# A hybrid decoder layer on one core: transfers ordered with few outstanding, squares on another engine, statistics by block, and one turn of the probabilities moved

## The chip, the cores and the metric

The kernel runs on one core of a Trainium2 chip. The core has TensorE (PE, the matrix multiplications), VectorE (DVE), ScalarE (ACT) and GpSimd (POOL), and SyncE (SP), which issues the transfers; 16 DMA engines carry them out. The metric is the device time of one launch in microseconds.

## The reference

Input x has 2048 rows of 1024 numbers in fp32, mem has 256 rows. The layer computes:

```
h = rms_norm(x, mix_norm_g); z = h @ w_in
lru_x, lru_gate, conf_a, conf_b = split(z)              # 512 columns each
y_lru = rg_lru(causal_dwconv(lru_x, 4 taps)) * gelu(lru_gate)
c = conf_a * sigmoid(conf_b)
c = silu(layer_norm(causal_dwconv(c, 31 taps)))
x = x + concat([y_lru, c]) @ w_out
q = rms_norm(x, xa_norm_g) @ w_q ; k, v = split(rms_norm(mem, mem_norm_g) @ w_kv)
x = x + softmax(q k^T / 16) v @ w_o                     # 4 heads of 256
g, u = split(rms_norm(x, ffn_norm_g) @ w_up)            # 3072 columns each
x = x + (gelu(causal_dwconv(g, 3 taps)) * u) @ w_down
return rms_norm(x, final_norm_g)
```

`rms_norm` divides a row by the root of the mean of its squares and multiplies by a gain; `rg_lru` is a gated linear recurrence along the rows, with two small matrix products for its gates.

## The kernel before, in words

**Numbers and products.** Every fp32 operand of a product is held as two rounded parts, `xh` and `xl` for activations, `wh` and `wl` for weights; ACT rounds (`yh<-s`), and DVE forms the rest (`yl<-s,yh`). `mm3` (line 636) turns one product into three matmuls. Large products are done as seven products of quarter blocks instead of eight (`seven`, line 1178, with the orders FIRST, SECOND and THIRD at 1153 to 1157), and the sums and differences of blocks that this needs (`t`, `s`, `raw`) are DVE's work; the weights' ones are stored in DRAM and read again.

**Stages.** The rows are done in four quarters `q` of 512 and two halves `h` of 1024. `mix_x` (771) loads a quarter of x, takes the sum of squares of its eight 128x512 blocks through `Stats.add` (on ACT, output `junk`), gets 1/rms from ACT's square root and DVE's reciprocal, scales the blocks on ACT (`x<-x,small`) and has PE turn them (`ps<-ident,x`). `memory_a` (1024) does the same for mem, and folds the key weights into w_q and the value weights into w_o. PE then makes z; the values `conf_a * sigmoid(conf_b)` are the tile `sg`, which goes to the DRAM tensor `zc` and comes back with its 30 earlier columns as `z<-zc` for the 31-tap convolution (`conv`, 893). There ACT writes the first tap of three sums (`e<-z`, `so<-z`, `f<-so`), and DVE adds the other taps, `e<-z,v,e` and its kin: this convolution is DVE's largest work in the first third. The recurrence (`lru`) has the tiles `xc`, `gate`, `m`. `attend(h)` (1323) makes three products with `seven`: FIRST (the output projection, into x), SECOND (the scores), and THIRD (probabilities by folded values). Row `score` (around 1388) of SECOND writes or adds to `prob`, and `softmax` exponentiates it on ACT (`prob,small<-prob,...`, with a row sum), takes a reciprocal on DVE and scales on ACT (`prob<-prob,small`). `turn` has PE transpose a block (`ps<-ident,prob`), and ACT copies it out (`pt<-ps`); from `pt` ACT and DVE make the parts `yh` and `yl` of the third product. The dictionary given to `seven` tells after which step (product n, block i) such a side task goes: before, the quarter `(0,0)` of the probabilities is turned after (3, 3), the end of the fourth of the seven score products. The feed-forward part (`feed_forward`, 1790) is a long even run of products with transfers beside them; `finish` (1742) squares the result, takes the statistics of the four blocks `tb` of 512 rows together, and scales and stores them.

**The order.** No engine's order is written by hand. The functions only record operations with what they read and write (`Program`, line 162); tasks are generators that `drive` (537) steps. `deadlines` (277) gives each operation a due time, worked back from PE's order; `schedule` (308) is a list scheduler which, whenever an engine is free in its model, starts the ready operation that is due first, with 85 tile slots S, 4 W, 3 D and 8 PSUM banks. This is repeated PASSES times, and the best of the orders by its own model is emitted. All transfers are issued by SP in one order; an SP entry that waits for its data holds up those behind it, as an ACT or DVE entry does on its engine.

Of the kernel before, what the change touches and what calls it, by code (L numbers as in the profile page):

```python
# [11 lines left out]
F32 = mybir.dt.float32  # L12
F32R = mybir.dt.float32r
AF = mybir.ActivationFunctionType
ALU = mybir.AluOpType
AX = mybir.AxisListType

P = 128
S = 2048
D = 1024  # L20
# [5 lines left out]
NTB = TT // P  # L26
# [12 lines left out]

SLOTS = dict(S=85, W=4, D=3, ps=8)
WIDTH = dict(S=TT, W=1024, D=1152, ps=TT)


# [8 lines left out]
ACT_SWITCH = 1.3  # L54
ACT_PATIENCE = 8.0
POOL_LAST = 6.0
PASSES = 3
STACKS = 2


# [88 lines left out]

class Op:  # L150
    __slots__ = ("eng", "idx", "calls", "cost", "delay", "sets", "preds", "succs", "bufs", "due",
                 "wait", "at", "start", "either", "on", "turn", "store", "first")

    def __init__(self, eng, idx):
        self.eng, self.idx = eng, idx
        self.calls, self.cost, self.delay, self.sets = [], 0.0, 0.0, None
        self.preds, self.succs, self.bufs = set(), [], []
        self.due, self.wait, self.at, self.start, self.either, self.on = 1e9, 0, 0.0, None, False, eng
        self.turn, self.store, self.first = 0.0, False, False


class Program:
# [114 lines left out]
    def deadlines(self, order):  # L277

        t = 0.0
        for o in self.ops:  # L280
            o.due, o.start, o.at = 1e9, None, 0.0
        for o in order:
            if o.eng == "PE":
                o.due = o.turn = t
                t += o.cost
            elif o.store:
                o.due = t + 30
        for o in reversed(self.ops):
            lat = o.cost + o.delay + HOP
            for s in o.succs:  # L290
                o.due = min(o.due, s.due - lat)
            for s in self.extra.get(o.idx, ()):
                if s.idx > o.idx:
                    o.due = min(o.due, s.due - lat)
            if o.first:
                o.due = o.idx - 1e6
        for _ in range(STACKS):
            for e in ("DVE", "ACT", "SP"):
                t = 1e9
                for o in sorted((o for o in self.ops if o.eng == e and not o.first), key=lambda o: -o.due):  # L300
                    t = o.due = min(o.due, t - o.cost)
            for o in reversed(self.ops):
                lat = o.cost + o.delay + HOP
                if o.eng != "PE" and not o.first:
                    for s in o.succs:
                        o.due = min(o.due, s.due - lat)

    def schedule(self):
# [6 lines left out]
        table, dma_free, lag = [None], [0.0], [0.0]  # L315
        order = []

        def push(t, kind, x):
            seq[0] += 1
            heapq.heappush(events, (t, seq[0], kind, x))  # L320
# [49 lines left out]
        def dispatch(e, t):  # L370
            if not idle[e]:
                return
            o = pick(e, t)
            if o is None:
                return
            idle[e] = False
            o.start, o.on = t, e
            order.append(o)
            if e == "PE":
                lag[0] += 0.2 * (t - o.turn - lag[0])  # L380
            cost = o.cost
            if e == "ACT" and o.sets is not None and table[0] not in o.sets:
                cost += ACT_SWITCH
                table[0] = o.sets[0]
            if o.either and e == "DVE":
                cost = estimate("DVE", "tensor_tensor", 1024, False)
            if e == "SP":
                dma_free[0] = max(dma_free[0], t) + cost
                push(t + 0.1, 2, e)
                push(dma_free[0] + o.delay, 0, o)  # L390
            else:
                push(t + cost, 2, e)
                push(t + cost, 0, o)
# [12 lines left out]
        while events:  # L406
            t, _, kind, o = heapq.heappop(events)
# [67 lines left out]
def hybrid_layer(  # L475
# [8 lines left out]
    cpool = ctx.enter_context(tc.tile_pool(name="cpool", bufs=1))  # L484
# [8 lines left out]
    pr = Program(nc, place)  # L493

    def const(shape, name, dtype=F32):
        return Buf(None, shape, cpool.tile(list(shape), dtype, name=name), dtype, name)

    def V(name, *a, **k):
        pr.do("DVE", name, *a, **k)

    def ACT(out, in_, func, **k):
        pr.do("ACT", "activation", out, in_, func, **k)
# [17 lines left out]
    def tmp(name="tmp"):  # L520
        return pr.new("S", name=name)
# [41 lines left out]
    eps = Buf(None, (P, 1), eps_t)  # L563
# [6 lines left out]
    gtail = zeros(NF, FK - 1, "gtail")  # L570
    hlast = zeros(NC4, 1, "hlast")

    n_small = [0]

    def small(w):
        n_small[0] += 1
        return const((P, w), f"small{n_small[0]}")


    def columns(rows, width, name):  # L580
# [119 lines left out]
    class Columns:  # L700
# [6 lines left out]
        def get(self, c0, kq):  # L707
# [10 lines left out]
                        self.kept.put(base + 2 * f + i, flat(got[f][i]))  # L718
            return got

    class Stats:
        def __init__(self):
            self.ss = small(2 * NTB)

        def add(self, tb, half, src):
            i = half * NTB + tb
            ACT(tmp("junk")[:], src, AF.Square, accum_out=self.ss[:, i : i + 1])

        def rstd(self):
            r = small(NTB)  # L730
# [6 lines left out]
    def turn(p, xs, k):  # L737
        with together():
            for tb in range(NTB):
                transpose(p[:, tb * P : (tb + 1) * P], xs[tb][k // 4][:, (k % 4) * P : (k % 4 + 1) * P], ident[:])  # L740
# [30 lines left out]
    def mix_x(h):  # L771
        if h:
            yield mixed_in[0]
        for q in range(2 * h, 2 * h + 2):
            xs = load_x(q, "x")
            st = Stats()
            for tb in range(NTB):
                for half in range(2):
                    st.add(tb, half, xs[tb][half][:])
            r = st.rstd()  # L780
            for half in range(2):
                for tb in range(NTB):
                    t = xs[tb][half]
                    ACT(t[:], t[:], AF.Copy, scale=r[:, tb : tb + 1])
            yield 0
            X = []
            MX[h].append(X)

            def take(k, p):
                hi, lo = pair("x")  # L790
                split_scaled(p[:], vec["v1024"][:, k, G_MIX : G_MIX + 1], hi[:], lo[:])
                X.append((hi, lo))

            yield from turned(xs, take, 1)
            del xs, X

    class Rowed:
# [6 lines left out]
        def put(self, c, q, src):  # L804
            self.tok[c, q] = Buf(None, (1,))
            pr.dma(self.t[c * P : (c + 1) * P, q * TT : (q + 1) * TT], src, writes=[self.tok[c, q]])

        def get(self, out, c, t0, n):
            toks = [self.tok[c, q] for q in range(t0 // TT, (t0 + n - 1) // TT + 1)]
# [214 lines left out]
    def memory_a():  # L1024
        pr.first = True
        xs = []
        for mb in range(2):
            parts = []
            ssp = small(2)
            for half in range(2):  # L1030
                t = tmp("mem")
                pr.dma(t[:], mem[0, mb * P : (mb + 1) * P, half * TT : (half + 1) * TT])
                ACT(tmp("junk")[:], t[:], AF.Square, accum_out=ssp[:, half : half + 1])
                parts.append(t)
            r = small(1)
            V("tensor_tensor", r[:], ssp[:, 0:1], ssp[:, 1:2], op=ALU.add)
            ACT(r[:], r[:], AF.Sqrt, bias=eps[:], scale=1.0 / D)
            V("reciprocal", r[:], r[:])
            for t in parts:
                ACT(t[:], t[:], AF.Copy, scale=r[:, 0:1])  # L1040
            xs.append(parts)
# [281 lines left out]
    def attend(h, ready):  # L1323
# [25 lines left out]
        def turn(src, th, half, take):  # L1349
            for k in range(KH):  # L1350
                p = ps()
                with together():
                    for tb in range(NTB):
                        transpose(p[:, tb * P : (tb + 1) * P], src[th, tb, half][:, k * P : (k + 1) * P], ident[:])
                take(th, half, k, p)
# [37 lines left out]
        def take_p(th, half, k, p):  # L1393
# [5 lines left out]
            (0, 1): [lambda: turn(xs, 1, 0, take), rates],  # L1399
            (1, 3): pass_on(1).get(0, ()),  # L1400
            (3, 0): pass_on(1).get(1, ()),
            (3, 3): [lambda: turn(prob, 0, 0, take_p)],
        })
        del X
        st2 = [Stats(), Stats()]
# [336 lines left out]
    def finish(h, acc):  # L1742
        g = []
        for half in range(2):
            t = tmp("gfin")
            pr.dma(t[:], final_norm_g[half * TT : (half + 1) * TT].partition_broadcast(P))
            g.append(t)
        for th in range(2):
            st = Stats()
            for tb in range(NTB):  # L1750
                for half in range(2):
                    st.add(tb, half, acc[th, tb, half][:])
            r = st.rstd()
            for tb in range(NTB):
                r0 = (2 * h + th) * TT + tb * P
                for half in range(2):
                    t = acc[th, tb, half]
                    V("scalar_tensor_tensor", t[:], t[:], r[:, tb : tb + 1], g[half][:], op0=ALU.mult, op1=ALU.mult)
                    pr.dma(out[0, r0 : r0 + P, half * TT : (half + 1) * TT], t[:])
            yield 1  # L1760

# [107 lines left out]
```

## Time and profile before

| | |
|---|---|
| median of three runs | 2477.26 us (2477.25 to 2478.92) |
| profiled execution | 2480.82 us, of which its span is 2479.0 us |
| PE busy | 2411.2 us (97%), 10788 matmuls |
| DVE busy | 1915.0 us (77%), 3187 instructions |
| ACT busy | 1290.1 us (52%), 2259 instructions |
| DMA moved | 572.06 MB, mean 231 GB/s |

The span is the time from the first to the last instruction of the profiled execution; 1.8 us of its time lie outside of it, and this execution took 3.6 us more than the median. PE is busy for 97% of the span, so the 67.8 us in which it is idle, and the stretches in which its clock is below full, are all that a change of order can win, as long as the matmuls stay the same. Almost all instructions are recorded by one helper, so all carry line 447; they are told apart by their tiles (`ps<-ident,prob` is the turn of the probabilities). In a row of the trace, a bracket at the end is the idle time of that engine before the instruction, and what ended it.

### The profile page before, as it was taken

How to read it: one execution, taken by the hardware profiler on the slowest of the kernel's cores; microseconds unless marked ns; L12 is line 12 of the kernel's file. 1: busy time of each engine (PE TensorE's matmuls, PEld its weight loads, DVE VectorE, ACT ScalarE, POOL GpSimd, SP SyncE). 2: the span in 40 equal slices, each digit the busy share in tenths (PEclk: the TensorE clock that was granted, in tenths of full speed). 3: DMA queues.
4: the chain of work that ended last, by engine and by line, in shares of the span. 5: the costliest groups of instructions: out<-in, count | busy, mean ns of one | idle time of the engine just before them, and what ended most of it. 6: DMA issues, size and time to landing. Idle time of an engine off the chain costs nothing.

```text
span 2479.0 us, 32376 instructions
## 1 busy us (share of the span) xinstructions
PE 2411.2 (97%) x10788; PEld 1986.0 (80%) x10788; DVE 1915.0 (77%) x3187; ACT 1290.1 (52%) x2259; POOL 0.7 (0%) x6
## 2 busy tenths in 40 slices
PE   6999999999989999999999999999999999999998
PEld 5888868877767888778888888888888888888886
DVE  4559979999989635696889888988786685667665
ACT  8427669266977655666545445554454441233222
POOL 0000000000000000000000000000000000000000
PEclk8999999999999999999999999999999999999999
DMA  7977678897796966565665446654542387769774
GB/s 252 378 274 239 217 234 301 267 336 244 234 313 219 374 228 229 157 218 187 235 228 188 171 173 206 223 181 160 173 143 77 102 303 257 257 223 374 255 244 156
DMA packets 339837, 572.06 MB, mean 231 GB/s; under 512 B 32924, under 2 KB 106652, under 8 KB 339670
## 3 DMA queue, kind: packets, MB, share of 16 engines
q1 hardware_dynamic: 339670, 570.00, 67.8%
q8 instruction: 85, 1.39, 0.2%
q14 instruction: 82, 0.67, 0.1%
HBM read 385.32 MB, written 184.55 MB: 230 GB/s over the span
## 4 chain that ended last, share of the span: by engine, by line
PE 68%; DVE 6%; ACT 3%; DMA 1%; issue 1%; SPq 0%; DVEq 0%; ACTq 0%
PE ps L447 68%; ACT prob L447 2%; DVE yl L447 1%; DVE s L447 1%; DVE t L447 1%; DVE gate L447 0%; DVE x L447 0%; DMA wh<-w_out 0%; DMA VO<-yh 0%; DVE Xl L447 0%; ACT yh L447 0%; DVE small L447 0%; DVE prob L447 0%; DVE xc L447 0%; DVE wl L447 0%
## 5 line engine op out<-in xcount | busy, mean ns | idle before, releaser
L447 PE MATMUL ps<-Xh,wh 128*128 128x512 f32 x1344 | 523.9, 390 | 1.1 <-DVE gb L447 0.9
L447 PE MATMUL ps<-Xh,wl 128*128 128x512 f32 x1344 | 523.2, 389 | 0.5 <-DVE wl L447 0.5
L447 PEld LDWEIGHTS ps<-Xh,wh 128*128 128x128 f32 x1344 | 252.3, 188 | 53.9 <-issue 1.3
L447 PEld LDWEIGHTS ps<-Xh,wl 128*128 128x128 f32 x1344 | 252.3, 188 | 53.3 <-DVE wl L447 1.1
L447 PE MATMUL ps<-wh,yh 128*128 128x512 f32 x672 | 268.7, 400 | 11.1 <-ACT yh L447 5.0
L447 PE MATMUL ps<-wh,yl 128*128 128x512 f32 x672 | 265.3, 395 | 2.0 <-DVE yl L447 2.0
L447 PE MATMUL ps<-wl,yh 128*128 128x512 f32 x672 | 264.9, 394 | 0.0
L447 PE MATMUL ps<-wh,hidh 128*128 128x512 f32 x672 | 261.4, 389 | 0.0
L447 PE MATMUL ps<-wl,hidh 128*128 128x512 f32 x672 | 261.4, 389 | 0.0
L447 DVE TENSOR_TENSOR acc<-acc,ps 128x512 f32<-128x512 f32 x192 | 129.2, 684 | 151.4 <-PE ps L447 150.6
L447 PE MATMUL ps<-wh,hidl 128*128 128x512 f32 x624 | 242.7, 389 | 0.0
L447 PE MATMUL ps<-Xl,wh 128*128 128x512 f32 x576 | 224.3, 389 | 1.3 <-DVE Xl L447 1.2
L447 PE MATMUL ps<-xh,wh 128*128 128x512 f32 x512 | 201.7, 394 | 0.0
L447 PE MATMUL ps<-xh,wl 128*128 128x512 f32 x512 | 199.3, 389 | 0.0
L447 PE MATMUL ps<-xl,wh 128*128 128x512 f32 x512 | 199.3, 389 | 0.0
L447 ACT ACTIVATE wh<-s 128x512 fp32r<-128x512 f32 x192 | 120.3, 629 | 133.0 <-DVE s L447 94.4
L447 PEld LDWEIGHTS ps<-wh,yh 128*128 128x128 f32 x672 | 128.5, 191 | 39.9 <-ACT yh L447 5.9
L447 ACT ACTIVATE u<-ps 128x512 f32<-128x512 f32 x144 | 85.6, 595 | 128.4 <-PE ps L447 127.7
L447 PEld LDWEIGHTS ps<-wh,yl 128*128 128x128 f32 x672 | 128.2, 191 | 30.3 <-DVE yl L447 3.0
L447 ACT ACTIVATE wh<-raw 128x512 fp32r<-128x512 f32 x176 | 108.3, 626 | 81.9 <-PE ps L447 43.0
L447 PEld LDWEIGHTS ps<-wl,yh 128*128 128x128 f32 x672 | 128.5, 191 | 27.0 <-issue 0.8
L447 PE MATMUL ps<-xn,wh 128*128 128x512 f32 x384 | 149.4, 389 | 0.0
(208 smaller groups left out, 4546.6 us busy)
## 6 DMA issues: line engine op xcount, KB each, us to landing
raw<-in_w_up_dram SPq DMA_DIRECT2D x96, 512.0 KB
wh<-w_down SPq DMA_DIRECT2D x164, 256.0 KB
wl<-w_down SPq DMA_DIRECT2D x164, 256.0 KB
hid<-cv SPq DMA_DIRECT2D x48, 512.0 KB
h<-hid SPq DMA_DIRECT2D x96, 256.0 KB
w_down<-wh SPq DMA_DIRECT2D x84, 256.0 KB
x<-in_x_dram SPq DMA_DIRECT2D x64, 256.0 KB
wh<-w_out SPq DMA_DIRECT2D x56, 256.0 KB
```

Source lines behind the costliest of these rows:

```text
L447: getattr(e, name)(*[resolve(a) for a in args], **{k: resolve(a) for k, a in kw.items()})
```

## The change

The diff has six parts.

- **Planner.** PASSES goes from 3 to 12. In `deadlines` the due times of PE's operations come from their starts in the schedule before instead of the sum of PE's costs. In `schedule`, SP takes up its next transfer only when the model's backlog of transfers is at most BACKLOG = 4 us. This rule stands in the planner's model only; the emitted kernel has no wait for it.
- **Early stores.** The stores of `sg` to `zc` get a due time that is 40 us earlier.
- **Small tiles.** About a hundred small constants become columns of one tile `smalls`, and the room gives one more slot (S 86).
- **Squares.** The sums of squares of the first quarter of x (8) and of half of each block of mem (2) go to DVE, as `scalar_tensor_tensor` with an accumulated sum, instead of ACT's `Square`.
- **Last norm.** `finish` takes its statistics for each block of 128 rows, not for four together.
- **Turn.** The first quarter of the probabilities is turned after (6, 0), the first block of the seventh score product, instead of after (3, 3).

```diff
-SLOTS = dict(S=85, W=4, D=3, ps=8)
+SLOTS = dict(S=86, W=4, D=3, ps=8)
...
-PASSES = 3
+PASSES = 12
+BACKLOG = 4.0
+EARLY_STORE = 40.0
+SMALLS = 720
...
-        for o in self.ops:
-            o.due, o.start, o.at = 1e9, None, 0.0
         for o in order:
             if o.eng == "PE":
-                o.due = o.turn = t
+                t = o.due = o.turn = t if o.start is None else o.start
                 t += o.cost
-            elif o.store:
-                o.due = t + 30
+            else:
+                o.due = t + 30 if o.store else 1e9
+        for o in self.ops:
+            o.start, o.at = None, 0.0
         for o in reversed(self.ops):
             lat = o.cost + o.delay + HOP
+            if o.early:
+                o.due -= EARLY_STORE
...
             if e == "SP":
                 dma_free[0] = max(dma_free[0], t) + cost
-                push(t + 0.1, 2, e)
+                push(max(t + 0.1, dma_free[0] - BACKLOG), 2, e)
...
     def small(w):
-        n_small[0] += 1
-        return const((P, w), f"small{n_small[0]}")
+        at, n_small[0] = n_small[0], n_small[0] + w
+        assert n_small[0] <= SMALLS, n_small
+        return Buf(None, (P, w), smalls[:, at : at + w], F32, f"small{at}")
...
+    def square(src, total, vector):
+        if vector:
+            V("scalar_tensor_tensor", tmp("junk")[:], src, 1.0, src, op0=ALU.mult, op1=ALU.mult, accum_out=total)
+        else:
+            ACT(tmp("junk")[:], src, AF.Square, accum_out=total)
...
-                    st.add(tb, half, xs[tb][half][:])
+                    st.add(tb, half, xs[tb][half][:], q == 0)
...
+            pr.ops[-1].early = self is zc
...
-                ACT(tmp("junk")[:], t[:], AF.Square, accum_out=ssp[:, half : half + 1])
+                square(t[:], ssp[:, half : half + 1], half == 1)
...
-            (3, 3): [lambda: turn(prob, 0, 0, take_p)],
+            (6, 0): [lambda: turn(prob, 0, 0, take_p)],
...
         for th in range(2):
-            st = Stats()
             for tb in range(NTB):
+                ss, r = small(2), small(1)
                 for half in range(2):
-                    st.add(tb, half, acc[th, tb, half][:])
-            r = st.rstd()
-            for tb in range(NTB):
+                    square(acc[th, tb, half][:], ss[:, half : half + 1], False)
+                V("tensor_tensor", r[:], ss[:, :1], ss[:, 1:], op=ALU.add)
+                ACT(r[:], r[:], AF.Sqrt, bias=eps[:], scale=1.0 / D)
+                V("reciprocal", r[:], r[:])
...
-                    V("scalar_tensor_tensor", t[:], t[:], r[:, tb : tb + 1], g[half][:], op0=ALU.mult, op1=ALU.mult)
+                    V("scalar_tensor_tensor", t[:], t[:], r[:], g[half][:], op0=ALU.mult, op1=ALU.mult)
```

The emitted orders show it at three places. The first is ACT at the start of the program, before: `junk<-x` are the squares of x, `small_97` and `small_109` the square roots for the first and the second quarter, `x<-x,small` the scaling, `xh<-ps` the rounding of the turned x.

```order
20 L447 ACTIVATE kv<-ps 128x256
21 L447 ACTIVATE small_97<-small_97,eps 128x4
22 L447 ACTIVATE junk,small_108<-x 128x512
23 L447 ACTIVATE kv<-ps 128x256
24 L447 ACTIVATE x<-x,small_97 128x512 x4
25 L447 ACTIVATE junk,small_108<-x 128x512
26 L447 ACTIVATE x<-x,small_97 128x512
27 L447 ACTIVATE xh<-ps,v_95 128x512 x2
28 L447 ACTIVATE junk,small_108<-x 128x512
29 L447 ACTIVATE x<-x,small_97 128x512 x3
30 L447 ACTIVATE xh<-ps,v_95 128x512
31 L447 ACTIVATE junk,small_108<-x 128x512
```

The same place on ACT in the changed kernel:

```order
5 L452 ACTIVATE mem<-mem,smalls 128x512 x4
6 L452 ACTIVATE mt<-ps,v_96 128x256 x8
7 L452 ACTIVATE smalls<-smalls,eps 128x4
8 L452 ACTIVATE x<-x,smalls 128x512 x7
9 L452 ACTIVATE xh<-ps,v_96 128x512 x2
10 L452 ACTIVATE x<-x,smalls 128x512
11 L452 ACTIVATE xh<-ps,v_96 128x512
12 L452 ACTIVATE junk,smalls<-x 128x512
13 L452 ACTIVATE xh<-ps,v_96 128x512
14 L452 ACTIVATE junk,smalls<-x 128x512
```

The squares of the first quarter are gone from ACT, all eight scalings of it stand right behind the square root, and the squares of the second quarter come behind them.

The second place is ACT where the first product of the recurrence's input ends (`z<-ps`) and the 31-tap convolution begins (`e<-z`, `so<-z`, `f<-so`), before:

```order
89 L447 ACTIVATE yh<-raw 128x512
90 L447 ACTIVATE sg<-ps 128x512 x4
91 L447 ACTIVATE wh<-raw 128x512 x8
92 L447 ACTIVATE z<-ps 128x512
93 L447 ACTIVATE e<-z,v_102 128x512
94 L447 ACTIVATE so<-z,v_102 128x513
95 L447 ACTIVATE f<-so,fast 128x512
96 L447 ACTIVATE e<-z,v_102 128x512
97 L447 ACTIVATE z<-ps 128x512 x2
```

And in the changed kernel:

```order
84 L452 ACTIVATE yh<-t 128x512
85 L452 ACTIVATE wh<-raw 128x512
86 L452 ACTIVATE e<-z,v_97 128x512
87 L452 ACTIVATE wh<-raw 128x512
88 L452 ACTIVATE so<-z,v_97 128x513
89 L452 ACTIVATE f<-so,fast 128x512
90 L452 ACTIVATE wh<-raw 128x512
91 L452 ACTIVATE z<-ps 128x512
92 L452 ACTIVATE wh<-raw 128x512
93 L452 ACTIVATE z<-ps 128x512
```

Before, the convolution's first taps stand behind `z<-ps`; now they stand ahead of it.

The third place is ACT in the third product of the second half (`attend(1)`), where four blocks of turned probabilities are copied out (`pt<-ps` x4) of which the next parts `yh<-s` are made, before; `prob,small_230<-prob` and its like are the last eight exponentials.

```order
783 L447 ACTIVATE prob,small_230<-prob,small_229,small_177 128x256
784 L447 ACTIVATE prob,small_227<-prob,small_226,small_177 128x256
785 L447 ACTIVATE prob,small_224<-prob,small_223,small_177 128x256
786 L447 ACTIVATE prob,small_221<-prob,small_220,small_177 128x256
787 L447 ACTIVATE prob,small_230<-prob,small_229,small_177 128x256
788 L447 ACTIVATE prob,small_227<-prob,small_226,small_177 128x256
789 L447 ACTIVATE prob,small_224<-prob,small_223,small_177 128x256
790 L447 ACTIVATE prob,small_221<-prob,small_220,small_177 128x256
791 L447 ACTIVATE pt<-ps 128x512 x4
792 L447 ACTIVATE prob<-prob,small_230 128x256
793 L447 ACTIVATE prob<-prob,small_227 128x256
794 L447 ACTIVATE prob<-prob,small_224 128x256
```

And in the changed kernel:

```order
679 L452 ACTIVATE pt<-ps 128x512
680 L452 ACTIVATE yh<-pt 128x512 x3
681 L452 ACTIVATE prob,smalls<-prob,smalls 128x256 x4
682 L452 ACTIVATE pt<-ps 128x512 x4
683 L452 ACTIVATE prob,smalls<-prob,smalls 128x256 x3
684 L452 ACTIVATE yh<-s 128x512 x2
685 L452 ACTIVATE prob,smalls<-prob,smalls 128x256
686 L452 ACTIVATE yh<-s 128x512 x4
687 L452 ACTIVATE prob<-prob,smalls 128x256 x8
688 L452 ACTIVATE yh<-s 128x512 x6
```

Before, eight exponentials stand directly ahead of the four `pt<-ps`; now four do, and four others come behind.

More of the change, by code (lines that the diff above doesn't have):

```diff
@@ L151 @@
     __slots__ = ("eng", "idx", "calls", "cost", "delay", "sets", "preds", "succs", "bufs", "due",
-                 "wait", "at", "start", "either", "on", "turn", "store", "first")
+                 "wait", "at", "start", "either", "on", "turn", "store", "first", "early")
     def __init__(self, eng, idx):
@@ L158, in __init__ @@
         self.due, self.wait, self.at, self.start, self.either, self.on = 1e9, 0, 0.0, None, False, eng
-        self.turn, self.store, self.first = 0.0, False, False
+        self.turn, self.store, self.first, self.early = 0.0, False, False, False
 class Program:
@@ L571, in hybrid_layer @@
     hlast = zeros(NC4, 1, "hlast")
+    smalls = cpool.tile([P, SMALLS], F32, name="smalls")
     n_small = [0]
     def small(w):
-        n_small[0] += 1
-        return const((P, w), f"small{n_small[0]}")
+        at, n_small[0] = n_small[0], n_small[0] + w
+        assert n_small[0] <= SMALLS, n_small
+        return Buf(None, (P, w), smalls[:, at : at + w], F32, f"small{at}")
     def columns(rows, width, name):
@@ L723, in __init__, with add @@
             self.ss = small(2 * NTB)
-        def add(self, tb, half, src):
+        def add(self, tb, half, src, vector=False):
             i = half * NTB + tb
-            ACT(tmp("junk")[:], src, AF.Square, accum_out=self.ss[:, i : i + 1])
+            square(src, self.ss[:, i : i + 1], vector)
         def rstd(self):
```

## The prediction

> **What bounds it now.** I read the busy shares first, then PE's waits, then a table by stage. The shares, with the number of instructions:
>
> ```profile
> PE 2411.2 (97%) x10788; PEld 1986.0 (80%) x10788; DVE 1915.0 (77%) x3187; ACT 1290.1 (52%) x2259; POOL 0.7 (0%) x6
> ```
>
> In the table each row has a stretch and its length in us, the busy us of PE, PE's weight loads, DVE, ACT and POOL, the granted clock, DMA share and GB/s:
>
> ```profile
> 0.00:62.00 62.00, 40.06 (x203) 35.02 (x204) 29.19 (x122) 53.45 (x116) 0.70 (x6) 0.89 0.76 252
> 62.00:186.00 124.00, 124.00 (x565) 102.67 (x564) 68.86 (x125) 39.75 (x66) 0.00 (x0) 1.00 0.92 326
> 310.00:372.00 62.00, 62.00 (x228) 42.84 (x228) 44.66 (x74) 43.12 (x64) 0.00 (x0) 1.00 0.71 234
> 372.00:558.00 186.00, 184.61 (x811) 151.87 (x811) 184.25 (x286) 114.76 (x159) 0.00 (x0) 1.00 0.88 301
> 600.00:682.00 82.00, 76.51 (x353) 62.67 (x352) 81.64 (x142) 68.76 (x116) 0.00 (x0) 0.98 0.71 229
> 682.00:744.00 62.00, 53.92 (x233) 42.71 (x231) 51.83 (x101) 46.13 (x109) 0.00 (x0) 0.94 0.91 313
> 744.00:806.00 62.00, 56.73 (x250) 45.45 (x251) 59.72 (x100) 46.27 (x94) 0.00 (x0) 0.94 0.69 219
> 1550.00:2418.00 868.00, 868.00 (x3829) 718.82 (x3830) 640.03 (x999) 330.42 (x534) 0.00 (x0) 1.00 0.63 213
> 2418.00:2479.00 61.00, 48.97 (x217) 40.22 (x215) 34.73 (x57) 15.37 (x41) 0.00 (x0) 0.93 0.42 153
> ```
>
> From 1550 to 2418 PE has no idle time (868.00 of 868.00), so nothing that is reordered there can gain. Its idle time, 2479.0 - 2411.2 = 67.8 us, lies at the start (62 - 40.06 = 21.9), from 600 to 806 (5.5 + 8.1 + 5.3 = 18.9), at the end (12.0), and for the rest in single waits. DVE is busy for 184.25 of 186 us from 372 and for 81.64 of 82 from 600: there PE runs as fast as DVE lets it, while between 62 and 186 DVE was idle for 124 - 68.86 = 55 us. What PE waits for in all (total, times, longest):
>
> ```profile
> PE ps L447 <- ACT x L447: 9.5, 3, 7.5
> PE ps L447 <- ACT pt L447: 6.9, 3, 3.4
> ```
>
> A long wait costs more than itself. In these stretches the columns are length, PE busy, clock, DMA share, GB/s:
>
> ```profile
> 41.90:49.50 7.60, 7.56 (x27) 0.64 0.17 61
> 679.00:682.50 3.50, 3.32 (x8) 0.53 0.31 116
> 685.50:692.50 7.00, 6.05 (x16) 0.51 0.72 246
> 747.00:754.00 7.00, 5.24 (x8) 0.51 0.72 232
> 1013.30:1020.20 6.90, 6.11 (x14) 0.51 0.36 91
> ```
>
> After the long waits at 686, 748 and 1014 (rows below) the clock is halved for about 6.8 us, so each loses some 3.4 us more. The Trainium skill (TensorE: Matmul & The Clock Gate, Part 1: The HAM clock gate) has the clock halve after a window of about 3.4 us without work; the waits of 3.28 to 5.96 us agree, but 679 to 682.5 at 0.53 follows waits of under 2 us each, so that a shortened wait need not free the clock here.
>
> **The start: -7 us.** ACT and DVE, as the timeline has them (start, duration, and in brackets the idle time before and its cause), and PE:
>
> ```profile
> 21.20 0.62 ACT L447 ACTIVATE junk<-x 128x512 f32<-128x512 f32 x1
> 23.83 2.54 ACT L447 ACTIVATE x<-x,small 128x512 f32<-128x512 f32 x4
> 26.43 3.25 PE L447 MATMUL ps<-ident,x 128*128 128x128 f32 x16 [1.73 <-ACT x L447]
> 37.25 0.69 DVE L447 TENSOR_TENSOR t<-raw 128x512 f32<-128x512 f32 x1 [2.32 <-DMA raw<-in_w_out_dram]
> 39.12 0.17 DVE L447 RECIPROCAL small<-small 128x4 f32<-128x4 f32 x1
> 41.94 1.97 PE L447 MATMUL ps<-ident,x 128*128 128x128 f32 x8 [7.49 <-ACT x L447]
> ```
>
> One square takes 0.62 us of ACT; ten leave it, 6.2 us, and the second quarter's eight now stand behind the first quarter's scaling. PE's transposes at 26.43, which waited for that, can come up to 5 us earlier. For the second quarter the reciprocal stood at 39.12 behind a `t<-raw` that waited 2.32 us for a transfer; now it stands ahead of it, so `x<-x` can begin some 3 us earlier, and the 7.49 us wait shortens by that. The 24 small products of `kv,qt` now stand in this gap ahead of the second quarter's transposes, and the half clock of 41.9 to 49.5 (7.6 x 0.36 = 2.7 us lost) goes with the gap. 3 + 2.7 + 1 to 2 us of the other waits makes 7, with 3 (no clock, no fill) and 10 (both waits go) as ends. What DVE takes on, ten squares at about 0.77 us (1.54 for two `e<-z,v,e`, below), lies in its 33 idle us of this stretch, but for the eight on which the first square root hangs: these run as x lands, as ACT's did.
>
> **DVE's lead and the turn, 186 to 806: -8 us more.**
>
> ```profile
> 157.74 0.60 ACT L447 ACTIVATE z<-ps 128x512 f32<-128x512 f32 x1 [22.24 <-PE ps L447]
> ...
> 146.07 0.70 DVE L447 TENSOR_TENSOR so<-z 128x527 f32<-128x527 f32 x1
> ...
> 159.09 1.54 DVE L447 SCALAR_TENSOR_TENSOR e<-z,v,e 128x512 f32<-128x512 f32 x2 [12.32 <-ACT e L447]
> ```
>
> The convolution's data were there at 146 (`so<-z` reads them), but its first taps on ACT stood behind `z<-ps`, which waited 22.24 us for PE, and DVE waited 12.32 us for them. In the new order the taps are ahead of it, and the stores and loads of `zc` come earlier on SP; DVE can begin this work 13 us earlier for the one reason and up to 22 us, at about 137, with the other. But this lead can't all be kept: between 310 and 372 DVE is idle for 17.3 us already, because the second half's products are not there, and a DVE that is early waits longer. So past 372 I count PE's own 7 us, 2 to 5 us for second-half products that stand a little earlier in PE's order, and nothing for the rest: a lead of about 10 at 682. DVE's added squares (7.7 us) are paid in idle time ahead of that.
>
> From 682 to 744 DVE is not full (51.83 of 62); ACT is late:
>
> ```profile
> 686.45 0.80 PE L447 MATMUL ps<-wh,yh 128*128 128x512 f32 x1 [3.28 <-ACT yh L447]
> 731.69 1.14 PE L447 MATMUL ps<-ident,prob 128*128 128x128 f32 x8 [2.54 <-ACT pt L447]
> 748.76 3.78 PE L447 MATMUL ps<-sum,ones 128*128 128x512 f32 x4 [5.96 <-DVE sum L447]
> ```
>
> With the turn after (6, 0), ACT's work ahead of these parts of `yh` is some ten operations of 0.5 to 0.6 us less, which is the first two waits (5.8 us, and 3.4 of clock). What is late next is DVE's `sum` at 748.76; its work ahead is the same, so I keep 5 of the 9 us. In all 15 us are won by 806, the start's 7 among them: 8 more. Ends: 0 more (DVE's path as long as now) and 22 more, if the idle 18.9 us, 3 of those ahead of 600, and 8 us of clock (3.4 + 3.4 + 1.6) go but for 8.
>
> **The second half's attention: -6 us.**
>
> ```profile
> 1008.78 0.60 ACT L447 ACTIVATE prob<-prob,small,small 128x256 f32<-128x256 f32 x1
> ...
> 1013.46 2.03 ACT L447 ACTIVATE pt<-ps 128x512 f32<-128x512 f32 x4
> 962.27 1.23 PE L447 MATMUL ps<-ident,prob 128*128 128x128 f32 x8 [1.45 <-ACT xt L447]
> ...
> 1014.09 0.79 PE L447 MATMUL ps<-wh,yh 128*128 128x512 f32 x1 [3.44 <-ACT pt L447]
> ```
>
> These eight exponentials ((1013.46 - 1008.78) / 8 = 0.58 us each) hold up `pt`, for which PE waits until 1014.09 (3.44 us), with 3.4 us of clock behind it. Four of them now come after `pt`: 2.3 us, and ACT is relieved of the moved turn ahead of it. I count 5 of the 6.8 us, and 1 of the 1.45 us at 962, next to the turn's old place. Ends 1 and 8.
>
> **The tail: -4 us.**
>
> ```profile
> 2467.01 0.69 DVE L447 TENSOR_TENSOR acc<-acc,ps 128x512 f32<-128x512 f32 x1 [0.71 <-PE ps L447]
> ...
> 2469.22 5.39 DVE L447 SCALAR_TENSOR_TENSOR acc<-acc,small,gfin 128x512 f32<-128x512 f32 x8
> ```
>
> Eight scalings of 5.39 / 8 = 0.67 us follow the last sum; by blocks of 128 rows six of them go ahead of it, and two remain: -4.0, less a little for four small statistics where there was one, which stand in idle time. Ends 3 and 5. The slots, the packed small tiles and the planner's passes move nothing else that has a price: PE has the same 10788 matmuls.
>
> **Sum.** 2480.8 - 7 - 8 - 6 - 4 = 2456 for a profiled execution; the median of before is 3.6 below its profile, so 2477.3 - 25 = 2452.
>
> **Rivals.**
> 1. DVE keeps its lead: the second half's work that is ready early fills 310 to 372, and the waits and half clocks up to 806 go nearly all (22 instead of 8): 2477.3 - 7 - 22 - 6 - 4 = 2438. For it: 55 us of idle DVE time ahead. Against: the 17.3 idle us at 310 to 372.
> 2. The middle stays: DVE's chain from 372 to 779 ends as late as now, eating the start's 7 too, and only the tail's 4, the 6 around 1000 are left: 2477.3 - 10 = 2467.
> 3. The change does little: ACT's waits are taken over by DVE at the same places (at 1014 DVE's `s<-pt` is as near), and the tail alone shows: 2474.
> 4. Slower, by late transfers. With few outstanding, SP's order brings each load close to its use; the planner's wait isn't in the kernel, but the order is.
>
> ```profile
> 393.51 0.38 SPq L447 DMA_DIRECT2D wl<-w_in  x1
> ...
> 399.71 0.39 PE L447 MATMUL ps<-xh,wh 128*128 128x512 f32 x1
> ...
> wl<-w_in SPq DMA_DIRECT2D x28, 256.0 KB
> ```
>
> This weight part, one of 28 from 360 to 530, is used by the group of matmuls at 399.71, 6.2 us after its issue, with the DMA engines at 0.88 share. If about 2 MB more stood ahead of it, at 301 GB/s that is 6.6 us: PE would then wait for each pair. At 1 us for 28 pairs, and four half clocks of 3.4 us (14 us), with start and tail still won (11): 2477 + 28 + 14 - 11 = 2508; it decides from about 1.9 MB on (6.2 x 301). In the new order the loads that PE reads directly stand at most 1.8 MB later, mostly under 1. The Trainium skill (DMA: Bandwidth & Descriptors, Rules for kernel authors) says to issue a transfer early and wait for it late, which speaks against this part of the change; the trace agrees only where the share is near 1.
>
> **How the numbers follow.** Forecast 2452 (2443 to 2461): 0.55. Rival 1, 2430 to 2443: 0.16. Rival 2, 2461 to 2472: 0.16. Rival 3, within 5 us (0.2%, about what a measurement of this kernel can tell): 0.07. Rival 4: 0.06. The range 2432 to 2471 leaves out 0.13 of rivals 3 and 4 and a little of the others. Faster 0.87, same 0.07, slower 0.06.
>
> **What would show it.** Right: the second quarter's transposes at 35 to 39 instead of 41.94; DVE's first `e<-z,v,e` before 147; no wait over 2 us at 686 or 1014 and the clock at 1.0 there; two scalings behind the last sum. Wrong: DVE full again from 372 to 779 with a wait for `sum` over 6 us; PE waiting for a DMA between 372 and 558; PE's busy time, now 2411.2, up by more than the clock explains.

## The result, and the profile after

The changed kernel takes 2453.62 us (median of 4 runs, 2452.36 to 2454.62) against 2477.72 us for the kernel before in the same runs: a ratio of 0.9901, 95% interval 0.9887 to 0.9915, which is 24 us less. Its profiled execution took 2454.62 us with a span of 2452.8 us, 26.2 us less than the span of before. The two traces differ by 2 us more than the medians do, because the profiled execution of before was a long one (2480.82 us against its median of 2477.72 us; after, 2454.62 us against 2453.62 us).

Busy time of the changed kernel by engine, with the number of instructions:

```profile
PE 2404.8 (98%) x10788; PEld 1982.3 (81%) x10788; DVE 1925.6 (79%) x3231; ACT 1281.6 (52%) x2250; POOL 0.7 (0%) x6
```

The matmuls are the same in number. PE's idle time fell from 67.8 to 2452.8 - 2404.8 = 48.0 us, and its busy time by 6.4 us, as fewer of the same matmuls ran at half clock (the mean granted clock is 0.993, before 0.989). DVE took over 10.6 us, ACT lost 8.5 us.

The table by stage for the changed kernel (columns: stretch and length, busy us of PE, PE's weight loads, DVE, ACT and POOL, granted clock, DMA share, GB/s):

```profile
0.00:62.00 62.00, 46.39 (x239) 40.00 (x240) 40.46 (x145) 52.41 (x103) 0.70 (x6) 0.94 0.78 251
310.00:372.00 62.00, 62.00 (x243) 45.49 (x242) 46.48 (x72) 44.61 (x66) 0.00 (x0) 1.00 0.74 245
372.00:558.00 186.00, 184.45 (x821) 152.35 (x820) 184.09 (x291) 106.61 (x154) 0.00 (x0) 1.00 0.88 302
558.00:600.00 42.00, 42.00 (x195) 35.01 (x194) 42.00 (x69) 29.91 (x58) 0.00 (x0) 1.00 0.90 303
600.00:682.00 82.00, 77.34 (x338) 61.94 (x337) 81.47 (x140) 67.02 (x106) 0.00 (x0) 0.96 0.74 243
682.00:744.00 62.00, 49.19 (x206) 37.46 (x205) 55.87 (x110) 57.00 (x129) 0.00 (x0) 0.89 0.82 288
744.00:806.00 62.00, 61.76 (x281) 51.16 (x280) 52.40 (x91) 43.17 (x91) 0.00 (x0) 1.00 0.80 269
```

PE is 6.3 us busier in the first 62 us, full from 558 to 600 and nearly full from 744 to 806, but from 682 to 744 it is idle for 12.8 us, more than the 8.1 us of before. The waits there and behind, from PE's timeline:

```profile
555.90 1.96 PE L452 MATMUL ps<-ident,x 128*128 128x128 f32 x16 [1.55 <-DVE x L452]
...
708.47 1.11 PE L452 MATMUL ps<-ident,prob 128*128 128x128 f32 x4 [4.60 <-ACT prob L452]
...
726.42 1.13 PE L452 MATMUL ps<-sum,ones 128*128 128x512 f32 x2 [2.83 <-DVE sum L452]
...
729.55 2.08 PE L452 MATMUL ps<-sum,ones 128*128 128x512 f32 x2 [2.00 <-DVE sum L452]
...
737.38 1.85 PE L452 MATMUL ps<-ident,prob 128*128 128x128 f32 x12 [1.44 <-ACT prob L452]
...
994.46 0.79 PE L452 MATMUL ps<-wh,yh 128*128 128x512 f32 x1 [2.89 <-ACT pt L452]
```

The waits of before at 574, 677, 686, 694 and 962 are gone. The one at 708 is new: PE reaches the turn of the block (1, 1) at the head of the third product before ACT has its probabilities done. The clock in the stretches around it (length, PE busy, clock, DMA share, GB/s):

```profile
656.00:664.00 8.00, 7.39 (x18) 0.57 0.73 264
685.50:692.50 7.00, 7.00 (x33) 1.00 0.73 255
705.00:712.00 7.00, 3.05 (x11) 0.68 0.75 255
724.00:732.00 8.00, 3.58 (x6) 0.75 0.62 221
990.00:1000.00 10.00, 7.11 (x33) 0.83 0.53 163
```

Where before had half clock from 686 there is full clock, and the loss is at 656, 705 and 724 instead. At 656 it follows three waits of 1.56, 1.84 and 0.64 us between 651 and 657, two of them for DVE's `yl` and `prob`; from 600 to 682 the clock is 0.96, before 0.98.

I took the same matmul in both traces and how much earlier it starts: 8.2 us from 62 to 240, 10.1 us at 500, 18.0 us at 600, 25.8 us at 700, but 16.8 us from 775 to 930; then 21.0 us at 1050, 21.6 us from 1550 on, and with the tail 26.2 us. At 700, though, before has done the turn and the changed kernel has it still ahead; behind the turn of both, at 720, the lead is 24.1 us. So 24 us were won by then, and 7 of them were given back in the next 50 us. One trace against one trace is not exact: e1 (below), whose time is that of before, is ahead of the trace of before by 1.3 us at 600 and 3.1 us at 1050, and e3, which changes the tail alone, by 1.6 and 1.2 us. A stage's share of the gain is known to some 1 to 3 us only.

### The profile page after: what moved, and what is told of

It reads as the page before. It is cut to its first block, busy times and chain, and to the rows that moved or that the text cites. A ratio compares the mean times of both kernels' runs of the same rounds, so it can differ in the third digit from the quotient of the medians.

```text
span 2452.8 us, 32183 instructions
## 1 busy us (share of the span) xinstructions
PE 2404.8 (98%) x10788; PEld 1982.3 (81%) x10788; DVE 1925.6 (79%) x3231; ACT 1281.6 (52%) x2250; POOL 0.7 (0%) x6
## 4 chain that ended last, share of the span: by engine, by line
PE 92%; DVE 3%; ACT 2%; DMA 1%; issue 1%; SPq 0%; DVEq 0%; ACTq 0%
PE ps L452 92%; ACT prob L452 1%; ACT L452 0%; DMA raw<-in_w_q_dram 0%; DVE Xl L452 0%; DVE s L452 0%; DVE acc L452 0%; DVE gate L452 0%; SPq L452 0%; DVE wl L452 0%; DVE yl L452 0%; DVE x L452 0%; DVE e L452 0%; ACT yh L452 0%; DVE conv L452 0%
## 5 line engine op out<-in xcount | busy, mean ns | idle before, releaser
L452 DVE TENSOR_TENSOR wl<-s,wh 128x512 fp32r<-128x512 f32 x192 | 130.5, 685 | 24.4 <-ACT wh L452 17.9
```

Of the source, the lines that this page charges most:

```text
L452: getattr(e, name)(*[resolve(a) for a in args], **{k: resolve(a) for k, a in kw.items()})
```

## The experiments

Each run was timed against the kernel before on the same chip. "Planned anew" means that the planner made the whole order again; "order kept" means that the edit acts on the finished order. All ratios are to the kernel before; the changed kernel's is 0.9901.

**e1_conv_early.** The finished order of the kernel before, with the first `z<-ps` on ACT put behind the convolution's first taps:

```diff
+        first = next(o for o in order if o.eng == "ACT" and out_name(o) == "z")
+        gate = next(o for o in order if o.eng == "ACT" and out_name(o) == "f")
+        order = delay(order, pre, first, gate)
```

Here `delay` puts `first`, and what depends on it up to there, right behind `gate`.

> The kernel before with three ACT instructions moved and nothing else: the first taps of the 31-tap convolution (e<-z, so<-z, f<-so) stand ahead of the first z<-ps instead of behind it. In both theories DVE's first e<-z,v,e starts at about 149 us instead of 159. Theory A (the prediction's: such a lead is lost where DVE waits for the second half's products between 310 and 372): no more than 2 us faster, 2475 to 2478. Rival B (DVE's chain from here sets the pace to 779): 8 to 12 us faster, about 2467.

Measured: 2477.97 us, ratio 0.9997 (0.9988 to 1.0006). DVE's group of this operation in that run (ns min/median/max, first and last start), DVE's next long wait, the stretch from 310 to 372, and PE's longest waits in the middle:

```profile
L451 DVE SCALAR_TENSOR_TENSOR e<-z,v,e x120: 735/748/759, 146.4 to 640.4; 128x512 f32<-128x512 f32 x120
```

```profile
164.03 0.69 DVE L451 TENSOR_TENSOR wl<-raw,wh 128x512 fp32r<-128x512 f32 x1 [10.13 <-ACT wh L451]
```

```profile
310.00:372.00 62.00, 62.00 (x229) 42.90 (x228) 44.66 (x74) 43.10 (x64) 0.00 (x0) 1.00 0.72 234
```

```profile
685.05 0.79 PE L451 MATMUL ps<-wh,yh 128*128 128x512 f32 x1 [3.31 <-ACT yh L451]
...
746.87 3.78 PE L451 MATMUL ps<-sum,ones 128*128 128x512 f32 x4 [5.11 <-DVE sum L451]
```

The convolution starts 12.7 us earlier (146.4 for 159.1), DVE is busy for the same 44.66 us between 310 and 372, and PE's waits of 3.3 and 5 us are where they were. The time is theory A's, but not its reason: the lead is gone long before 310. DVE, in its order, comes to a `wl` for which ACT has no `wh` yet and waits 10.13 us for it; of the 12.7 us only 2.3 us more of DVE's work are done by 186, and 0.6 us by 310. Rival B's time falls, but what a lead that lasts to 310 would be worth this run doesn't show.

**e2_conv_late.** The changed kernel's order kept, with the three taps put behind the first `z<-ps`:

```diff
+        gate = next(o for o in order if o.eng == "ACT" and out_name(o) == "z")
+        for n in ("f", "so", "e"):
+            order = delay(order, pre, next(o for o in order if o.eng == "ACT" and out_name(o) == n), gate)
```

> The changed kernel with its order kept, but the convolution's first taps on ACT, and what hangs on them, put behind the first z<-ps again, as before. DVE's first e<-z,v,e at about 151 us instead of 140.5. Theory A: no more than 2 us slower than the changed kernel, 2453 to 2456. Rival B: about 10 us slower, 2463.

Measured: 2452.10 us, ratio 0.9886 (0.9871 to 0.9901); DVE's first `e<-z,v,e` at 150.0. Nearly ten microseconds of lead given up cost nothing: theory A's time again. Here too the lead ends before 310. The changed kernel, which starts at 140.5, loses it to waits for ACT, of 1.93 us at 178 and this one:

```profile
189.65 0.69 DVE L452 TENSOR_TENSOR gate<-gate,xc 128x512 f32<-128x512 f32 x1 [4.86 <-ACT gate L452]
```

These waits are absent in e2, and between 140 and 310 DVE does 160.8 us of work in the one and 160.5 us in the other.

**e3_tail_only.** The kernel before with the statistics by block in `finish`, as in the diff of the change. Planned anew.

```diff
-            st = Stats()
...
+                ss, r = small(2), small(1)
...
+                V("tensor_tensor", r[:], ss[:, :1], ss[:, 1:], op=ALU.add)
+                ACT(r[:], r[:], AF.Sqrt, bias=eps[:], scale=1.0 / D)
+                V("reciprocal", r[:], r[:])
```

> The kernel before with the last norm's statistics taken for each block of 128 rows, nothing else. Theory A (only two scalings are left behind the last sum): 4 to 5 us faster, 2473. Rival C (the stores behind the scalings set the end, and they end as late): within 1 us of before, 2477.

Measured: 2475.22 us, ratio 0.9983 (0.9974 to 0.9992), which is 4.2 us (2.0 to 6.4). Theory A; rival C falls. The changed kernel's tail shows the two scalings behind the last sum, where before had eight in 5.39 us:

```profile
2445.38 0.69 DVE L452 TENSOR_TENSOR acc<-acc,ps 128x512 f32<-128x512 f32 x1
...
2448.22 1.41 DVE L452 SCALAR_TENSOR_TENSOR acc<-acc,smalls,gfin 128x512 f32<-128x512 f32 x2
```

**e4_turn_back.** The changed kernel with the turn in its old place, planned anew:

```diff
-            (6, 0): [lambda: turn(prob, 0, 0, take_p)],
+            (3, 3): [lambda: turn(prob, 0, 0, take_p)],
```

> The changed kernel with the first turn of the probabilities after (3, 3) again; the order is planned anew. Theory A (the turn's move relieves ACT in both attention stages): 8 to 10 us slower than the changed kernel, 2462, with waits for ACT at the sixth product's parts and near 960. Rival D (what the move wins in the first half is lost to the waits for the exponentials at 708 and 737): 2452 to 2456.

Measured: 2458.31 us, ratio 0.9914 (0.9900 to 0.9927): 3 us slower than the changed kernel by the ratios, 4.7 by the medians, between the two forecasts, with intervals that overlap. PE's waits for the turn in this run, in the first and the second half:

```profile
675.35 3.68 PE L452 MATMUL ps<-ident,prob 128*128 128x128 f32 x16 [10.20 <-ACT prob L452]
...
945.61 1.80 PE L452 MATMUL ps<-ident,prob 128*128 128x128 f32 x12 [1.25 <-ACT xt L452]
```

In its old place the turn makes PE wait 10.20 us in one piece, but the wait of 4.6 us at 708 isn't there then. Both theories seem half of it: the place of the turn decides where PE waits for the softmax, and moving it shifts some of the wait and saves the rest.

**e5_squares_act.** The changed kernel's order kept; the ten squares are emitted on ACT where they stood:

```diff
+                    if name == "scalar_tensor_tensor" and "accum_out" in kw:
+                        e, name, args, kw = self.engines["ACT"], "activation", (args[0], args[1], AF.Square), dict(accum_out=kw["accum_out"])
```

> The changed kernel with its order kept, but the ten squares given to ACT at the places where they stood, as before. Ten times 0.61 us come back on ACT ahead of the first quarter's square root. Theory A (the squares' move is what brings the first quarter's transposes 5 us earlier and wins most of the start's 8 us): 4 to 6 us slower than the changed kernel, 2458 to 2460. Rival F (PE waits for the transfer of w_q at 32.6 us anyway, 4.84 us, and the order alone wins the start): no more than 1 us slower, 2454.

Measured: 2457.35 us, ratio 0.9912 (0.9899 to 0.9926), slower by 2.7 us by the ratios, whose intervals overlap, and by 3.7 us by the spans (2456.5 against 2452.8); by 62 us its trace is 3.3 us behind. ACT's square root of the first quarter and the scaling behind it in this run, and, in the fence after, in the changed kernel:

```profile
20.30 0.30 ACT L454 ACTIVATE smalls<-smalls,eps 128x4 f32<-128x4 f32 x1
20.84 4.40 ACT L454 ACTIVATE x<-x,smalls 128x512 f32<-128x512 f32 x7 [0.24 <-DVE smalls L454]
```

```profile
16.12 0.30 ACT L452 ACTIVATE smalls<-smalls,eps 128x4 f32<-128x4 f32 x1
16.67 4.40 ACT L452 ACTIVATE x<-x,smalls 128x512 f32<-128x512 f32 x7 [0.24 <-DVE smalls L452]
...
32.59 1.94 PE L452 MATMUL ps<-ident,raw 128*128 128x128 f32 x8 [4.84 <-DMA raw<-in_w_q_dram]
```

The squares on DVE bring the square root forward by 4.2 us, and some 3 of these reach the end: less than theory A's 4 to 6, more than rival F's 1. The rest of the start's 8 us comes with the order around them. Rival F was right that a wait for w_q (4.84 us) stands behind, but it doesn't swallow them.

**e6_backlog_off, e7_passes3, e8_no_early.** The changed kernel planned anew with one constant set back in each:

```diff
-BACKLOG = 4.0
+BACKLOG = 1e9
...
-PASSES = 12
+PASSES = 3
...
-EARLY_STORE = 40.0
+EARLY_STORE = 0.0
```

> The changed kernel planned without the limit on outstanding transfers, all else as changed. Theory A (the gain comes from the orders of ACT, DVE and PE, not of SP): within 3 us of the changed kernel, 2451 to 2457. Rival G (the order of the transfers is the main part): 2462 to 2470.

> The changed kernel planned with 3 passes instead of 12. Theory A (the parts that are written in the code make the gain): within 4 us of the changed kernel, 2450 to 2458. Rival H (the longer search makes it): 2463 to 2475, with the waits of before at 574, 686 and 748 back.

> The changed kernel planned without the earlier due times of the zc stores. Theory A, as the two runs on the convolution's place have it (its start is worth nothing): within 2 us of the changed kernel, 2452 to 2456. Rival B: 6 to 10 us slower, 2460 to 2464.

Measured: without the limit on outstanding transfers 2461.66 us, ratio 0.9928 (0.9915 to 0.9942), 6.7 us slower than the changed kernel by the ratios; with 3 passes 2453.26 us, 0.9895 (0.9881 to 0.9908); without the early stores 2453.92 us, 0.9899 (0.9885 to 0.9912). So neither the longer search nor the earlier due times of the stores are worth anything that these intervals show (rival H falls). Without those due times the convolution began at 138.2, no later than in the changed kernel, so that run says nothing on rival B. The limit is worth about 7 us: outside theory A's range and at the edge of rival G's. A new plan alone doesn't make such a difference: the four of e7 to e10 take 2452.21 to 2454.70 us. In the run without it PE's stretch from 558 to 600 is broken again:

```profile
0.00:62.00 62.00, 44.33 (x225) 38.06 (x226) 36.80 (x138) 49.77 (x100) 0.70 (x6) 0.94 0.83 265
...
558.00:600.00 42.00, 38.25 (x172) 30.76 (x173) 42.00 (x71) 28.68 (x52) 0.00 (x0) 1.00 0.87 289
```

Against the changed kernel that is 2.1 us less PE work by 62, and 3.75 us less from 558 to 600. The waits there are for DVE and ACT (1.65, 1.16 and 1.69 us), not for transfers. Until 700 ACT waits 45 us for transfers, in the changed kernel 26 us; but in e9 below, which is as fast as the changed kernel, it waits 47.6 us. So the runs show that the limit pays, and not how: whether by the transfers' own order or by what the planner does with the other engines stays open. This run began the convolution at 118.9, 22 us ahead of the changed kernel. DVE had most of this lead still at 186 and lost it then, idle for 20.8 us from 186 to 310 (changed kernel 5.9 us) and for 26.3 us from 310 to 372 (15.5 us); the second of these is the loss that theory A of e1 had in mind.

**e9_old_due.** The changed kernel planned anew with PE's due times from summed costs:

```diff
-                t = o.due = o.turn = t if o.start is None else o.start
+                o.due = o.turn = t
```

> The changed kernel planned with PE's due times from the sum of its costs again, all else as changed. Theory A' (the limit on outstanding transfers is the planner's part that counts, about 7 us): within 3 us of the changed kernel, 2451 to 2457. Rival I (the due times from real starts are what took the waits at 574 and 686 away): 6 us slower or more, 2460, with a wait of over 3 us between 560 and 580 back.

Measured: 2452.21 us, ratio 0.9894 (0.9880 to 0.9908). The due times are worth nothing that shows; rival I falls.

**e10_third_later.** The changed kernel with the turn whose wait is new one block later in the third product, planned anew:

```diff
-            (0, 1): [lambda: turn(prob, 1, 1, take_p)],
...
-            (0, 2): norm_next(0, 1, 2),
+            (0, 2): [lambda: turn(prob, 1, 1, take_p)] + norm_next(0, 1, 2),
```

> The changed kernel with the turn of the block (1, 1) in the third product after its third block instead of its second, 2.7 us of products later, planned anew. If the wait of 4.6 us at 708 for the exponentials only takes back what PE had won there, it shrinks by about 2.7 us and its half clock goes: 3 to 5 us faster, 2449 to 2451. Rival J (the same wait appears at the next step, for pt or for sum): within 1 us of the changed kernel.

Measured: 2454.70 us, ratio 0.9902 (0.9887 to 0.9917), no gain. PE's waits in that run:

```profile
706.96 0.66 PE L452 MATMUL ps<-ident,prob 128*128 128x128 f32 x4 [0.77 <-ACT prob L452]
...
712.89 2.08 PE L452 MATMUL ps<-sum,ones 128*128 128x512 f32 x2 [3.89 <-DVE VO L452]
...
737.08 3.68 PE L452 MATMUL ps<-ident,prob 128*128 128x128 f32 x16 [4.36 <-ACT prob L452]
```

The wait of 4.6 us becomes 0.77 us, and waits of 3.89 and 4.36 us stand at the next steps: rival J. In this stretch ACT and DVE are both behind PE, and a single turn that is moved only shifts the wait.

**e11_turn_only.** The kernel before with the turn after (6, 0), nothing else, planned anew:

```diff
-            (3, 3): [lambda: turn(prob, 0, 0, take_p)],
+            (6, 0): [lambda: turn(prob, 0, 0, take_p)],
```

> The kernel before with the turn of the probabilities after (6, 0), nothing else, planned as before. Theory A (the move relieves ACT on its own): 4 to 6 us faster, 2473, with shorter waits at 686 and 1014. Rival D (on its own it is lost again to the exponentials or to sum at 748): within 2 us of before, 2477.

Measured: 2466.94 us, ratio 0.9961 (0.9948 to 0.9973): 9.7 us (6.7 to 12.9), twice what I expected. From 600 on, by stage, in this run (columns as above):

```profile
600.00:682.00 82.00, 79.72 (x367) 65.34 (x366) 81.21 (x138) 68.34 (x116) 0.00 (x0) 0.98 0.71 233
682.00:744.00 62.00, 50.67 (x216) 38.49 (x215) 58.05 (x120) 54.72 (x130) 0.00 (x0) 0.92 0.91 317
744.00:806.00 62.00, 60.15 (x279) 49.42 (x278) 56.03 (x91) 44.09 (x89) 0.00 (x0) 1.00 0.73 250
930.00:992.00 62.00, 62.00 (x300) 52.00 (x299) 38.55 (x79) 39.76 (x95) 0.00 (x0) 1.00 0.72 242
992.00:1054.00 62.00, 59.13 (x286) 49.49 (x285) 43.56 (x81) 38.02 (x91) 0.00 (x0) 1.00 0.62 201
```

The wait at 686 is gone, and that for `pt` in the second half is 2.87 us for 3.44. PE's busy time from 600 to 806 rises from 187.2 to 190.5 us, its clock from 744 to 806 goes from 0.94 to 1.00, and in the second half the stretch from 930 is full and the one from 992 at full clock (0.94 before): theory A, and rival D falls for the kernel before.

**e12_planner_only.** The kernel before with PASSES 12, the due times from starts and the limit on outstanding transfers; no step of the computation is changed:

```diff
+PASSES = 12
+BACKLOG = 4.0
...
+                t = o.due = o.turn = t if o.start is None else o.start
...
+                push(max(t + 0.1, dma_free[0] - BACKLOG), 2, e)
```

> The kernel before with the planner's three changes alone (12 passes, due times from starts, limit on outstanding transfers), no step of the computation moved or changed. Theory A' (the parts add up: 24 less 4 for the tail, 3 for the squares, 4 to 5 for the turn): 12 to 13 us faster, 2465. Rival K (the parts need each other): 5 us faster or less, 2473.

Measured: 2473.50 us, ratio 0.9980 (0.9971 to 0.9989), 5 us. PE's waits at the start and at the turn in this run:

```profile
28.84 3.67 PE L448 MATMUL ps<-ident,x 128*128 128x128 f32 x16 [4.58 <-ACT x L448]
...
48.68 3.68 PE L448 MATMUL ps<-ident,x 128*128 128x128 f32 x16 [4.76 <-ACT x L448]
...
687.08 3.67 PE L448 MATMUL ps<-ident,prob 128*128 128x128 f32 x16 [9.53 <-ACT prob L448]
```

The time is rival K's. Its order is 3.9 us ahead of before from 580 to 650; then the turn in its old place makes PE wait 9.53 us in one piece, and 2.0 us are left at 775. The start is as before (PE is busy for 40.99 of the first 62 us, before 40.06). But rival K's reason, that the parts need each other, does not follow: alone, the turn gives 9.7 us, the planner 5, the tail 4.2, and with 2.7 for the squares (e5) that makes 21.6 of the 24.5 us of the ratio. Theory A' fell because it had the turn at 4 to 5 us; with e11's 9.7 it would have said some 7, and the interval here is 2.7 to 7.2 us. The turn, which gives 9.7 us alone and 3 us in the changed kernel (e4), is the one part whose worth may depend on the others. The packed small tiles and the added slot were not tried on their own.

## Why the prediction was right

The time, 2452 against 2453.62 us, came from four stage totals that are each near; inside the middle one this is luck, as its errors offset each other.

- **Start: forecast 7, measured 8.2 us.** The squares on DVE and the order do it, as forecast (e5: 2.7 to 3.7 of it are the squares). The second quarter's transposes did not move, though: they start at 41.59 instead of 41.94, not at 35 to 39. In the changed kernel, and in the fence after it in the kernel before:

```profile
34.32 7.44 PE L452 MATMUL ps<-kv,qt 128*128 128x256 f32 x24
35.54 5.00 ACT L452 ACTIVATE x<-x,smalls 128x512 f32<-128x512 f32 x8
41.59 1.04 PE L452 MATMUL ps<-ident,x 128*128 128x128 f32 x8
44.20 2.78 PE L452 MATMUL ps<-ident,x 128*128 128x128 f32 x24
```

```profile
39.32 2.56 ACT L447 ACTIVATE x<-x,small 128x512 f32<-128x512 f32 x4 [1.75 <-DVE small L447]
52.44 2.78 PE L447 MATMUL ps<-ident,x 128*128 128x128 f32 x24
```

  "`x<-x` can begin 3 us earlier" was right (35.54 for 39.32), but "the wait shortens by that" was not: PE has the 24 products of `kv,qt` ahead, and the wait is gone. What the first quarter won is lost to the transfer of w_q at 32.59, which no term had: the same transposes of `raw` started at 33.05 before, so only 0.5 us are won by there. The other 7.7 us come with the filled gap, for which I had 5.7; the squares count here too, since in e5 PE waits 3.47 us for ACT's `qt` ahead of these products.
- **Middle: forecast 8 more, measured 16.8 - 8.2 = 8.6 us.** That DVE's lead from the convolution can't be kept was right, but the place was wrong: in e1 and in the changed kernel it is lost at DVE's next waits for ACT, at 164 and 190, and only of e6's lead of 22 us a part gets as far as the idle time from 310 to 372. DVE was full again from 372 to 682 (184.09 of 186, 42.00 of 42, 81.47 of 82 us), and PE gained there all the same; from 372 to 558 PE is itself busy for 184.61 of 186 us in the kernel before, so that "PE runs as fast as DVE lets it" was not shown by DVE's share. Two steps missed. I had a lead of 10 us at 682, and it was 18.0 us at 650 already: 5.9 us of that came at the wait at 574, which had no term in the forecast. And from there to 806 I had 5 us more, 9 from the turn less 4 for "DVE's `sum` next, its work ahead the same". The turn did remove the waits at 686 and 694 (e11) and the lead rose to 24.1 us, but then PE gave back 7.3, to its waits for `prob` at 708 and 737 (4.60 and 1.44 us), for `sum` (2.83 and 2.00 us) and to the clock, and at 806 it was 1.2 us less than at 650. I named `sum` and missed the softmax. An error of 8 us one way and one of 6 us the other cancelled, the first in part the start's.
- **Second half's attention: forecast 6, measured 21.0 - 16.8 = 4.2 us.** The wait at 962 is gone. The wait for `pt` at 1014 is not: 2.89 us for 3.44. Of "four of the eight exponentials now come after `pt`: 2.3 us" 0.6 us reached PE; what was won there is mostly clock (0.94 to 0.97 in the stretch from 992 to 1054). That part isn't the change's doing: e1 and e3, which change nothing there and wait 3.43 us each, have 0.97 in this stretch too.
- **Tail: forecast 4, measured 4.6 us** in the trace and 4.2 us alone (e3).
- **The planner.** "The planner's passes move nothing else that has a price" was right for the passes (e7). I gave the limit on outstanding transfers no gain of its own and a rival that speaks against it. It is the part of the planner that pays, about 7 us within the changed kernel (e6), in a way that the runs leave open. No loads came late in the changed kernel between 372 and 558, where PE is busy for 184.45 of 186 us; rival 4 did not happen. The rule of the Trainium skill that stood beside it (DMA: Bandwidth & Descriptors, Rules for kernel authors) does not decide here: behind the start, PE waits for a load in the changed kernel only once, 0.33 us at 649, so the loads are still issued early enough.

The wait at 574 and its half clock are 5.9 us of the gain. The wait (3.49 us, for ACT's `xa`) is gone with the planner alone (e12: no wait over 1.83 us between 558 and 600), and stays with the turn alone (e11: 3.48 us), so it is the planner that takes it away. The half clock behind it is another matter. The stretch in the kernel before, in e1 and in e11, all with this wait of 3.48 or 3.49 us:

```profile
569.00:580.00 11.00, 7.51 (x25) 5.71 (x24) 10.38 (x18) 10.79 (x20) 0.00 (x0) 0.69 0.94 302
```

```profile
569.00:580.00 11.00, 7.53 (x27) 5.72 (x26) 11.00 (x18) 10.38 (x20) 0.00 (x0) 0.84 0.96 332
```

```profile
569.00:580.00 11.00, 7.53 (x36) 5.71 (x35) 11.00 (x19) 10.88 (x21) 0.00 (x0) 1.00 0.94 311
```

The same wait cost much, some or none of the clock, so some 2 us of the 5.9 are an accident of the profiled execution of before. What stays open is how the limit on transfers wins its 7 us, and how much the turn is worth beside the other parts. None of the variants that were timed is faster than the changed kernel by more than the intervals.

## What to carry to other kernels

An engine that gets work done early wins only if its next inputs are also early: look for its next wait for another engine, and count the lead as lost there unless something fills it. Where three engines hand work round, a step that PE must not pass too early (here a transpose that waits for a softmax) sets the gain of all that lies ahead of it, so price its move together with the rest and look which wait comes next. Filling a gap of PE with products that are ready can be worth more than shortening the gap (here 7.7 us at a gap of 7.49 us, with the clock of the first 62 us at 0.94 for 0.89). And a half clock that follows one wait in one trace need not follow it in the next, so price the wait and call its clock a chance.

## What the runs showed of the hardware

A square with an accumulated sum cost DVE no more than the sums of two 128x512 tiles in these traces (0.69 us for `acc<-acc,ps`): the main instruction took 0.69 us, the accumulator's read-out 0.08 us, and one such pair followed another every 0.61 us, as ACT's did:

```profile
11.03 0.69 DVE L452 SCALAR_TENSOR_TENSOR junk<-x 128x512 f32<-128x512 f32 x1
11.64 0.08 DVE L452 DVE_READ_ACCUMULATOR junk<-x 128x1 f32 x1
11.64 0.69 DVE L452 SCALAR_TENSOR_TENSOR junk<-x 128x512 f32<-128x512 f32 x1
```

In the changed kernel the granted clock averaged 0.68 from 705 to 712, around a wait of 4.60 us, 0.75 from 724 to 732, where the waits were 2.83 and 2.00 us with short matmuls between, and 0.57 from 656 to 664, behind waits of 1.56, 1.84 and 0.64 us: several waits of under 3 us each cost clock as one long one does. And one wait of 3.48 or 3.49 us at 574 left 0.69, 0.84 or 1.00 from 569 to 580 in three runs.
